# The second mixer of a three-block kernel, issued in another order: convolution inputs among the latents and queries, forward transforms among the keys, the keys' norms last

## The chip, the cores and the metric

The kernel runs on one core of a Trainium2 chip. The metric is device time in microseconds (us) of one execution; the time given for a kernel is the median of several runs.

## The reference, cut to what matters

Three blocks are chained over one sequence of 512 positions with 1024 features, all in float32. The change lies in the first half of the second block, its mixer: latent attention with 8 heads beside a long convolution (Hyena), both from the same normed input. In short:

```python
def second_block(x, ...):
    h = _rmsnorm(x, norm_mix)
    c_q, c_kv, k_pe, u_h = split(h @ w_in)            # 768, 256, 32, 1536 columns
    q = (_rmsnorm(c_q, q_norm) @ w_uq)                # 8 heads x 96
    kv = (_rmsnorm(c_kv, kv_norm) @ w_ukv)            # 8 heads x (64 key + 64 value)
    k = concat([k_nope, k_pe broadcast to the heads])
    q, k = _rmsnorm(q, qk_norm_q), _rmsnorm(k, qk_norm_k)   # per head, then rotary part
    y_attn = softmax(q k^T / sqrt(96)) v

    u_h = _dwconv3(u_h, short_conv_w, short_conv_b)   # 3-tap convolution over time
    x0, x1, vh = split(u_h, 3)                        # 512 columns each
    y_hyena = x0 * _bidir_long_conv(x1 * vh, h_fwd, h_bwd, bias)   # by rfft / irfft

    y_mix = concat([_rmsnorm(y_attn, ...), _rmsnorm(y_hyena, ...)])
    x = x + y_mix @ w_out
```

## The kernel before, in words

Activations are kept transposed, features on the 128 partitions and the 512 positions along the row, so that a tile is 128x512 and the stream x is 8 such tiles. Float32 products are made of three matmuls: both operands are split into a high part (rounded to the type that TensorE takes) and a low remainder, and wh·ah, wl·ah and wh·al are added up in one bank of PSUM. `proj_T` makes one 128-column tile of a projection so, with 8 x 3 = 24 matmuls of 128x512; `proj_N` makes tiles that have positions on the partitions, with matmuls of 128x256, and hands each half bank to an evacuation function. Both take their bank from a ring of three, called mm. `w()` loads the weights (512 KB by a DMA of SyncE's queue, SP), casts the high part on ScalarE (ACT, L110) and subtracts for the low part on VectorE (DVE, L111; on GpSimd, POOL, for the two convolution tiles in `UG`).

Ahead of the mixer, `TwoNorms.finish` (L1155) scales the 8 tiles of x on DVE (L1168) and writes each to a scratch in DRAM by a DMA of ACT's queue (L1171, 256 KB each); x's memory then goes back to the allocator, and the mixer's tiles are placed on it.

`mix2` has these steps, with the names used below:

- **latents**: two tiles ckv and six tiles cq by `proj_T`. Each is split with its gain (`split_scaled`: high part ACT L192, low part DVE L193), and ACT squares it (L1246 for the first tile, L1249 after it) for the norm's factor. Both readers use the bank itself. Between them stands kpe, one tile of 32 columns, which ACT copies out (L1271).
- **keys(g)**, four, and **queries(g)**, three: `proj_N` over ckv and cq; ACT evacuates keys and queries, DVE the values v (L1294).
- **wave(i)**, four: two convolution tiles, `uh(8+i)` and `uh(4+i)`, each a `proj_T` followed by a factor (`times`, DVE L249) and the 3-tap convolution (`conv3`: ACT L1133, DVE L1135 and L1136); then their product u (DVE L1357) and its write to DRAM. **turned(i)** transposes u on TensorE and splits it (ACT, DVE L1347). **gate0(i)**, four, is a convolution tile that is only written out.
- **norms** of q and k per head: ACT squares, DVE sums (L1317), a power on POOL (`rsqrt`: DVE L231, POOL L232), DVE scales (L1323, L1327). The rotary part is `rotate` (L1225 to L1227).
- **forward(f)**, two: 24 matmuls of 128x512 over the turned u, a mirror step on DVE (L1124, L1125), then the product with the filter's spectrum on DVE (L1388, L1389, L1391) and POOL, and splits (ACT L183, DVE L185) into Y. **inverse(j)** transforms back.
- **attention**: per head transposes of q and k (L1444) and their splits (L192, L193), scores (three matmuls per 128 rows), maxima on DVE (L1459), exponentials on ACT (L1461), transposes of the probabilities (L1474) and the values' matmuls.

Before, the order in the program is: ckv, kpe, cq, keys, queries; the waves, with a norm of q and k in each; rotation, gate0(0), gate0(1), turned(3); then the attention heads, behind which a list `fill` is written: gate0(2), gate0(3), forward(0), forward(1), inverse(0), inverse(1). Each engine executes its own instructions in the order of its list. That order is set when the kernel is built by a scheduler that takes the program's order as priority and its own idea of when inputs are ready, so a step that is written later can fill a wait of an earlier one. Tiles come from pools that open and close with a scope (`m2a` for latents, `m2b` for the turned u, `m2d` for attention); a tile that is placed on memory that another tile had waits until that one's last reader is done.

Of the kernel before, what the change touches and what calls it, by code (L numbers as in the profile page):

```python
# [10 lines left out]
F32 = mybir.dt.float32  # L11
# [6 lines left out]
P = 128  # L18
# [1173 lines left out]
def mix2(k, h, r12, bc, kf, xp, x1, done):  # L1192
# [3 lines left out]
    with k.tc.tile_pool(name="m2", bufs=1) as p:  # L1196
# [41 lines left out]
        with k.tc.tile_pool(name="m2a", bufs=1) as pa:  # L1238
            def latent(nm, n, g):
                out, acc = [], None  # L1240
                for i in range(n):
                    ps = k.proj_T([k.aps[nm][i]], h)
                    out.append(k.split_scaled(k.pair(pa, f"{nm}{i}"), ps, k.v(g, i)))
                    if acc is None:
                        acc = pa.tile([P, T], F32, tag=nm + "a", name=k.name("sa"))
                        S.activation(out=acc, in_=ps, func=AF.Square)  # L1246
                    else:
                        sq = tmp()
                        S.activation(out=sq, in_=ps, func=AF.Square)  # L1249
                        G.tensor_tensor(out=acc, in0=acc, in1=sq, op=ALU.add)  # L1250

                ss = k.small()
                V.tensor_tensor(out=ss, in0=r12, in1=r12, op=ALU.mult)
                V.tensor_tensor(out=ss, in0=ss, in1=k.col_sums(acc), op=ALU.mult)
                r = k.rsqrt(ss, NT, 1.0 / (n * P))
                o = p.tile([P, NT], F32, tag=nm + "r", name=k.name("lr"))
                V.tensor_tensor(out=o, in0=r, in1=r12, op=ALU.mult)
                return out, o

            ckv, rkv = latent("w2ckv", 2, "kv_norm")  # L1260

            hi, lo = k.w(k.aps["w2kpe"], 256)
            ps = k.bank()
            for i in range(NK):
                a, b = h[i]
                s = slice(i * 32, i * 32 + 32)
                k.mm(ps[0:32], hi[:, s], a, i == 0, False)
                k.mm(ps[0:32], lo[:, s], a, False, False)
                k.mm(ps[0:32], hi[:, s], b, False, i == NK - 1)
            kp = pa.tile([32, T], F32, tag="kp", name="kp")  # L1270
            S.copy(out=kp, in_=ps[0:32])  # L1271
            cq, rq = latent("w2cq", 6, "q_norm")
            ps = k.bank("t", 2)
            for t in range(NT):
                nc.tensor.transpose(ps[:, t * 32 : t * 32 + 32], kp[:, t * P : (t + 1) * P], k.ident[0:32, 0:32])
# [1062 lines left out]
```

## Time and profile before

| | |
|---|---|
| median of 3 runs | 2282.41 us (2281.33 to 2283.66) |
| profiled execution, its own time | 2280.31 us |
| its span (first to last instruction) | 2278.5 us |
| mean granted TensorE clock | 0.986 |
| TensorE matmuls (PE) busy | 2216.6 us, 97% of the span |
| DVE busy | 1391.8 us, 61% |
| ACT busy | 939.0 us, 41% |
| POOL busy | 534.1 us, 23% |

The second mixer lies, in this execution, between about 680 us and 970 us. Times in the rows are microseconds from the span's start unless they are marked ns. In rows of instructions, `[3.34 <-ACT P L1461]` means that the engine sat idle for 3.34 us until ACT's instruction of line 1461 had written P. PEclk is the granted clock as a share of the full one. A matmul's own time in the rows overlaps its neighbours'; how fast TensorE goes is read from the distance of their starts.

### The profile page before, as it was taken

The page shows a single profiled execution, that of the slowest core. Times are in us where ns is not written, and L with a number is a line of the kernel's source. Part 1 is how long each engine was busy: PE and PEld are TensorE (multiplying, and loading weights), DVE is VectorE, ACT ScalarE, POOL GpSimd, SP SyncE. Part 2 cuts the span into 40 slices and gives each one's busy share as a digit, 9 for nine tenths or more (in the row PEclk, how much of TensorE's full clock was granted, in tenths as well). Part 3 has the DMA queues.
Part 4 walks back from the last instruction along what each step waited for, and adds up shares of the span by engine and source line. Part 5 has one row for each costly group of instructions (what it writes and reads, how often), then busy time and mean ns, then how long its engine had stood idle before and what let it go on. Part 6 is the DMA issues. An engine that isn't in the chain of part 4 may idle for free.

```text
span 2278.5 us, 29275 instructions
## 1 busy us (share of the span) xinstructions
PE 2216.6 (97%) x11180; PEld 1822.6 (80%) x11180; DVE 1391.8 (61%) x2228; ACT 939.0 (41%) x1579; POOL 534.1 (23%) x459
## 2 busy tenths in 40 slices
PE   7899899999999998999999999999999999999998
PEld 3677789888888985678888887888888888888886
DVE  8775576654354598579647647977766664433433
ACT  4444455542243446544324334455444323222221
POOL 5232554431122225231101103000111211210320
PEclk8999999999999999999999999999999999999999
DMA  9552312122333342133232243212222322223222
GB/s 333 158 159 83 101 56 75 56 70 89 102 103 105 112 137 64 63 123 99 80 115 93 79 141 126 93 66 84 88 90 87 130 84 95 100 77 117 93 82 75
DMA packets 82164, 232.59 MB, mean 102 GB/s; under 512 B 10047, under 2 KB 10944, under 8 KB 82025
## 3 DMA queue, kind: packets, MB, share of 16 engines
q1 hardware_dynamic: 67208, 205.49, 28.0%
q10 hardware_dynamic: 14816, 25.25, 3.4%
q8 instruction: 88, 1.44, 0.3%
q14 instruction: 52, 0.42, 0.1%
HBM read 215.99 MB, written 15.22 MB: 101 GB/s over the span
## 4 chain that ended last, share of the span: by engine, by line
PE 56%; DVE 2%; issue 2%; ACT 1%; POOL 0%; POOLq 0%; DVEq 0%; ACTq 0%
PE mm L116 49%; PE s L116 3%; PE o L116 2%; PE t L116 1%; DVE sg L1634 0%; PE t L1474 0%; ACT wh L110 0%; DVE wl L111 0%; DVE x L2304 0%; DVE B L193 0%; DVE x L1635 0%; DVE st L1459 0%; PE t L1989 0%; ACT A L192 0%; PE t L1952 0%
## 5 line engine op out<-in xcount | busy, mean ns | idle before, releaser
L116 PE MATMUL mm<-A,wh 128*128 128x512 f32 (+1 forms) x2192 | 693.2, 392 | 4.8 <-ACT k L702 3.8
L110 ACT CAST wh<-wr 128x1024 fp32r<-128x1024 f32 (+3 forms) x370 | 363.4, 984 | 630.6 <-PE mm L116 416.0
L111 DVE TENSOR_TENSOR wl<-wr,wh 128x1024 fp32r<-128x1024 f32 (+3 forms) x366 | 438.0, 1198 | 282.4 <-ACT wh L110 280.4
L116 PE MATMUL mm<-B,wh 128*128 128x512 f32 x1688 | 541.9, 397 | 3.6 <-DVE B L193 2.1
L116 PEld LDWEIGHTS mm<-A,wh 128*128 128x128 f32 (+1 forms) x2192 | 409.8, 188 | 91.0 <-ACT k L702 4.1
L116 PE MATMUL mm<-A,wl 128*128 128x512 f32 (+1 forms) x1096 | 430.1, 393 | 1.1 <-DVE wl L111 1.1
L116 PEld LDWEIGHTS mm<-B,wh 128*128 128x128 f32 x1688 | 316.6, 188 | 75.4 <-DVE B L193 3.7
L116 PE MATMUL mm<-B,wl 128*128 128x512 f32 x844 | 332.4, 394 | 0.0
L116 PEld LDWEIGHTS mm<-A,wl 128*128 128x128 f32 (+1 forms) x1096 | 206.0, 188 | 44.0 <-DVE wl L111 1.9
L116 PEld LDWEIGHTS mm<-B,wl 128*128 128x128 f32 x844 | 159.0, 188 | 34.0 <-issue 1.2
L116 PE MATMUL mm<-a,wh 128*128 128x512 f32 x448 | 140.4, 389 | 0.0
L232 POOL TENSOR_TENSOR r<-r,mhalf 128x4 f32<-128x4 f32 (+1 forms) x40 | 53.1, 1330 | 351.9 <-DVE r L231 351.9
L249 DVE TENSOR_TENSOR us<-mm,bc 128x512 f32<-128x512 f32 x95 | 65.2, 689 | 93.6 <-PE mm L116 92.6
L185 POOL TENSOR_TENSOR a<-sl,a 128x512 fp32r<-128x512 f32 x28 | 40.5, 1446 | 274.2 <-ACT a L183 274.2
L116 PEld LDWEIGHTS mm<-a,wh 128*128 128x128 f32 x448 | 84.1, 188 | 17.4
L116 PE MATMUL mm<-a,wl 128*128 128x512 f32 x224 | 86.8, 389 | 0.0
L116 PE MATMUL mm<-wh,A 128*128 128x256 f32 x448 | 84.6, 285 | 0.0
L116 PEld LDWEIGHTS mm<-wh,A 128*128 128x128 f32 x448 | 70.7, 191 | 1.1 <-issue 0.6
L2224 POOL TENSOR_TENSOR sl<-sl,bc 128x512 f32<-128x512 f32 x22 | 28.7, 1305 | 167.6 <-DVE sl L1580 167.6
L116 PE MATMUL mm<-wl,A 128*128 128x256 f32 x224 | 63.7, 285 | 1.0 <-DVE wl L111 1.0
L734 ACT ACTIVATE d<-d 128x512 f32<-128x512 f32 x56 | 35.1, 629 | 68.4 <-POOL d L733 68.4
L1609 DVE TENSOR_TENSOR x<-x,mm 128x512 f32<-128x512 f32 x32 | 22.0, 687 | 64.5 <-PE mm L116 64.5
(584 smaller groups left out, 3568.6 us busy)
## 6 DMA issues: line engine op xcount, KB each, us to landing
wr<-w2upg SPq DMA_DIRECT2D x22, 512.0 KB, 3.4
wr<-w2upu SPq DMA_DIRECT2D x22, 512.0 KB, 3.5
wr<-w3fg SPq DMA_DIRECT2D x22, 512.0 KB, 3.4
wr<-w3fu SPq DMA_DIRECT2D x22, 512.0 KB, 3.4
adar<-w1ada SPq DMA_DIRECT2D x32, 256.0 KB, 5.1
wr<-w3out SPq DMA_DIRECT2D x16, 512.0 KB, 3.5
wr<-w2uh SPq DMA_DIRECT2D x12, 512.0 KB, 3.5
wr<-w2dn SPq DMA_DIRECT2D x16, 384.0 KB, 3.0
```

The costliest lines, as they stand in the source:

```text
L110: nc.scalar.copy(out=hi[:, :n], in_=r[:, :n])
L111: (eng or nc.vector).tensor_tensor(out=lo[:, :n], in0=r[:, :n], in1=hi[:, :n].bitcast(F32), op=ALU.subtract)
L116: return self.nc.tensor.matmul(out, a, b, start=start, stop=stop)
L185: eng.tensor_tensor(out=l[:p], in0=src, in1=hi[:p].bitcast(F32), op=ALU.subtract)
L232: nc.gpsimd.tensor_tensor(out=r, in0=r, in1=self.mhalf[:, :n], op=ALU.pow)
L249: self.nc.vector.tensor_tensor(out=out, in0=ps, in1=bc, op=ALU.mult)
L734: nc.scalar.activation(out=d, in_=d, func=AF.Exp)
L1609: k.nc.vector.tensor_tensor(out=xs[n], in0=xs[n], in1=ps, op=ALU.add)
L2224: nc.gpsimd.tensor_tensor(out=s, in0=s, in1=norm.bc, op=ALU.mult)
```

## The change

The same instructions are issued in another order; the arithmetic is the same. The pool `m2b` is opened ahead of `m2a`, and `latent` becomes a class whose tiles and whose norm factor can be issued apart.

```diff
         un = [None] * NT
+        bp = k.ctx2.enter_context(k.tc.tile_pool(name="m2b", bufs=1))
+        B = lambda i: k.pair(bp, f"B{i}")
...
         with k.tc.tile_pool(name="m2a", bufs=1) as pa:
...
-            ckv, rkv = latent("w2ckv", 2, "kv_norm")
+            lkv, lq = Latent("w2ckv", 2, "kv_norm"), Latent("w2cq", 6, "q_norm")
+            lkv.tiles(2)
...
             S.copy(out=kp, in_=ps[0:32])
-            cq, rq = latent("w2cq", 6, "q_norm")
+            lq.tiles(3)
+            wave(0)
+            lq.tiles(3)
...
+            ckv, cq = lkv.out, lq.out
+            rkv, rq = lkv.factor(), lq.factor()
...
+            wave(1)
+            queries(0)
+            wave(2)
+            queries(1)
+            wave(3)
+            queries(2)
+            gate0(0)
+            normed(qh, 96, None)
+            for i in range(1, 4):
+                gate0(i)
+            rotate(qh[:, :, :, 64:80], qh[:, :, :, 80:96], tabs[0], 8)
+            turned(3, us[3])
+            keys(0)
+            keys(1)
+            forward(0)
+            keys(2)
+            keys(3)
+            normed(kt, 64, kpr)
+            forward(1)
+
         with k.tc.tile_pool(name="m2d", bufs=1) as pd:
...
             fill = [
-                lambda: gate0(2),
-                lambda: gate0(3),
-                lambda: forward(0),
-                lambda: forward(1),
                 lambda: inverse(0),
                 lambda: inverse(1),
             ]
```

`normed` makes the norms of all four row tiles of q, or of k, in two pairs; `wave`, `gate0`, `turned` and `forward` are the same code as before, moved up.

In the following rows each line is one instruction in an engine's list: line of the program, operation, output and inputs, size, and in brackets which engines or DMA queues it waits for.

ACT at the start of the mixer, before. `scr_x` is the scratch that the x tiles are written to, `bc` a broadcast factor that scales them:

```order
L192 ACTIVATE w2ckv_6050<-mm_6019,vec 128x512 [waits PE_49]
L110 CAST wh_6143<-wr_6141 128x1024 [waits DMAHW6_49]
L1246 ACTIVATE sa_6054<-mm_6019 128x512 [waits DVE_49]
L192 ACTIVATE w2ckv_6087<-mm_6056,vec 128x512 [waits PE_49]
L110 CAST wh_6180<-wr_6178 128x1024 [waits DMAHW7_49]
L1249 ACTIVATE tmp_6091<-mm_6056 128x512 [waits DVE_49]
L244 COPY bc_5969<-t_5964 128x512 [waits PE_49]
L244 COPY bc_5976<-t_5971 128x512 [waits PE_49]
L1171 DMA scr_x<-x_4687 128x512 [waits DVE_49]
L1271 COPY kp<-mm_6113 32x512 [waits PE_49]
```

The same place in the changed kernel (its lines 1343, 1346 and 1371 are the lines 1246, 1249 and 1271 of before):

```order
L1171 DMA scr_x<-x_4699 128x512 [waits DMAHW2_49,DVE_49]
L1171 DMA scr_x<-x_4701 128x512 [waits DMAHW3_49,DVE_49]
L192 ACTIVATE w2ckv_6053<-mm_6022,vec 128x512 [waits DMAHW4_49,DMAHW3_49,DMAHW5_49,DMAHW2_49,DMAHW6_49,DMAHW1_49,DMAHW7_49,DMAHW0_49,Activation_49]
L192 ACTIVATE w2ckv_6090<-mm_6059,vec 128x512
L1371 COPY kp<-mm_6103 32x512
L1343 ACTIVATE sa_6057<-mm_6022 128x512 [waits DVE_49]
L1346 ACTIVATE tmp_6094<-mm_6059 128x512 [waits DVE_49]
L192 ACTIVATE w2cq_6161<-mm_6130,vec 128x512 [waits PE_49]
```

The splits and squares of both ckv tiles and the copy of kpe now stand behind all eight write-outs of x, and the first split waits for all DMA queues.

TensorE at the end of kpe (mm_6103) and the start of the first cq tile (mm_6130), in the changed kernel:

```order
L116 MATMUL mm_6103<-A_5930,wh_6099 32x512
L116 MATMUL mm_6103<-A_5930,wl_6100 32x512
L116 MATMUL mm_6103<-A_5931,wh_6099 32x512
L116 MATMUL mm_6130<-A_5638,wh_6133 128x512 [waits Activation_49]
L116 MATMUL mm_6130<-A_5638,wl_6134 128x512
```

The order is that of before here (and the wait for ACT too): ckv, ckv and kpe take the three banks, and the cq tile takes the one that is free first.

DVE around the first scores, before (kT and qT are a head's transposed keys and queries, st the maxima of its scores):

```order
L111 TENSOR_TENSOR wl_8367<-wr_8364,wh_8366 128x1024 [waits DMAHW7_49,Activation_49]
L1135 SCALAR_TENSOR_TENSOR tmp_8186<-tmp_8185,vec,tmp_8186 128x511 [waits DMAHW0_49,Activation_49]
L1136 SCALAR_TENSOR_TENSOR tmp_8186<-tmp_8185,vec,tmp_8186 128x511 [waits DVE_49]
L193 SCALAR_TENSOR_TENSOR kT_7404<-t_7398,vec,kT_7403 96x512 [waits Activation_49]
L1124 TENSOR_TENSOR tmp_8221<-tmp_8220,mm_8213 128x512 [waits DMAHW6_49,PE_49,Activation_49]
L193 SCALAR_TENSOR_TENSOR qT_7448<-t_7442,gs,qT_7447 96x512 [waits Activation_49]
L1125 TENSOR_TENSOR tmp_8220<-tmp_8220,mm_8213 128x512 [waits DVE_49]
L1388 TENSOR_TENSOR ft_8244<-tmp_8220,tmp_8198 128x512 [waits DMAHW7_49,DVE_49]
L1459 TENSOR_REDUCE st_7413<-s_7414 128x1 [waits PE_49]
```

The same place in the changed kernel (L1255 and L1259 scale the keys, L1314, L1315 and L1317 are forward's products):

```order
L185 TENSOR_TENSOR A_7395<-ft_7379,A_7394 128x512 [waits Activation_49]
L1124 TENSOR_TENSOR tmp_7592<-tmp_7591,mm_7584 128x512 [waits PE_49]
L1255 TENSOR_TENSOR k<-k,r_7526 128x8x64 [waits Pool_49]
L1259 TENSOR_TENSOR k<-kpr,r_7526 128x8x32
L1314 TENSOR_TENSOR ft_7596<-tmp_7572,tmp_7550 128x512 [waits DMAHW6_49,DVE_49]
L111 TENSOR_TENSOR wl_8454<-wr_8451,wh_8453 128x1024 [waits DMAHW2_49,Activation_49]
L1125 TENSOR_TENSOR tmp_7591<-tmp_7591,mm_7584 128x512 [waits DVE_49]
L1255 TENSOR_TENSOR k<-k,r_7537 128x8x64 [waits Pool_49]
L1259 TENSOR_TENSOR k<-kpr,r_7537 128x8x32
L1315 TENSOR_TENSOR tmp_7550<-tmp_7591,tmp_7550 128x512 [waits DVE_49]
L1317 TENSOR_TENSOR tmp_7591<-tmp_7591,tmp_7551 128x512 [waits DMAHW7_49,DVE_49]
L193 SCALAR_TENSOR_TENSOR kT_7650<-t_7644,vec,kT_7649 96x512 [waits Activation_49]
```

In the order before, the first head's kT stands ahead of what DVE does for the two forward transforms; in the changed order all of forward(0), the mirror steps of forward(1) and the scaling of all four key tiles stand ahead of it. From the L249 of gate0(0) to this kT, DVE's list in the changed kernel has, beside it: 6 L111 of 128x1024 and 4 of 128x512; 4 each of L249, L1135 and L1136; 16 sums of the norms (8 of q, 8 of k) and 4 scalings each of q, of k and of k's rotary part; 4 instructions of the rotation; 16 evacuations of v; 8 mirror steps; 3 each of L1314 (two of them into ft), L1315 and L1317; 4 L185; 2 qT; and 17 short ones (4 low halves of the turned u and 13 of 8 columns or fewer).

More of the change, by code (lines that the diff above doesn't have):

```diff
@@ new lines, in turned @@
+        def turned(i, u):
+            ps = k.bank("t", 2)
+            for t in range(NT):
+                nc.tensor.transpose(ps[:, t * P : (t + 1) * P], u[:, t * P : (t + 1) * P], k.ident)
+            for t in range(NT):
+                if i == 0:
+                    un[t] = B(t)
+                s = slice(i * P, (i + 1) * P)
+                S.copy(out=un[t][0][:, s], in_=ps[:, t * P : (t + 1) * P])
+                V.tensor_tensor(
+                    out=un[t][1][:, s], in0=ps[:, t * P : (t + 1) * P], in1=un[t][0][:, s].bitcast(F32), op=ALU.subtract
+                )
@@ new lines, in mix2, with wave, normed @@
+        us = []
+        def wave(i):
+            a, b = uh(8 + i), uh(4 + i)
+            u = tmp()
+            V.tensor_tensor(out=halved(u), in0=turns(a), in1=turns(b), op=ALU.mult)
+            S.dma_start(out=su[i], in_=u)
+            us.append(u)
+            if i:
+                turned(i - 1, us[i - 1])
+        def normed(x, w, pe):
+            for t in range(0, NT, 2):
+                rs = [head_sums(x, w, pe, t + i) for i in range(2)]
+                for i in range(2):
+                    head_scale(x, w, pe, t + i, rs[i])
```

218 lines of the change are left out of this document (95 added, 123 removed).

## The prediction, on record before the result was known

> **What bounds the kernel now.** I read the page first: over the span TensorE (PE) is busy for 97%, so a change of order can only win or lose the few places where it is not. Then a table of windows over the second mixer, whose columns are the stretch, its length, the busy time (and count) of PE, PE's weight loads, DVE, ACT and POOL, then the granted clock and DMA:
>
> ```profile
> 688.00:775.00 87.00, 87.00 (x555) 77.24 (x555) 36.83 (x71) 36.15 (x66) 16.98 (x14) 1.00 0.33 107
> 775.00:836.00 61.00, 61.00 (x280) 50.45 (x279) 56.06 (x102) 27.61 (x51) 23.14 (x11) 1.00 0.37 121
> 836.00:900.00 64.00, 54.39 (x256) 37.34 (x255) 57.94 (x78) 39.34 (x80) 28.17 (x20) 0.92 0.32 99
> 900.00:968.00 68.00, 64.76 (x369) 47.24 (x369) 37.11 (x52) 40.19 (x78) 16.61 (x12) 1.00 0.19 63
> ```
>
> Latents, keys and queries (688 to 775) leave DVE idle more than half the time and PE never. From the waves to the third head (775 to 900) DVE is busy for 56.06 + 57.94 = 114.0 of 125 us: that stretch is DVE's, and in its second half PE stands for 64 - 54.39 = 9.6 us. After 900 it stands for 3.2 us more. One of these gaps is long enough to halve the clock. The next rows are two gaps of PE from the timeline (and between them the first scores), and windows of 4 us behind each gap:
>
> ```profile
> 74.81 1.84 PE L116 MATMUL mm<-ones,ada 128*128 128x1 f32 x8 [6.08 <-DVE ada L425]
> ...
> 844.61 0.63 PE L116 MATMUL s<-kT,qT 96*128 96x512 f32 x2
> ...
> 887.56 1.65 PE L116 MATMUL s<-kT,qT 96*128 96x512 f32 x3 [3.34 <-ACT P L1461]
> ...
> 76.00:80.00 4.00, 4.00 (x16) 3.69 (x16) 0.73 (x2) 1.32 (x3) 0.00 (x0) 0.50 0.41 131
> 80.00:84.00 4.00, 4.00 (x14) 2.34 (x12) 2.83 (x5) 4.00 (x8) 0.00 (x0) 0.75 0.00 0
> ...
> 892.00:896.00 4.00, 3.54 (x11) 2.46 (x11) 3.50 (x6) 3.04 (x7) 2.60 (x3) 0.50 0.29 113
> 896.00:900.00 4.00, 4.00 (x16) 1.60 (x15) 2.40 (x4) 1.72 (x4) 0.00 (x0) 0.78 0.00 0
> ```
>
> After 6.08 us of standing, PE runs at half clock from 74.8 until about 82 (0.75 over 80 to 84 is half of it at half): 7.2 us, in which 3.6 us of work are lost. After 3.34 us it does so from 887.6 to about 898, and 5 us are lost. So the mixer loses 9.6 + 3.2 + 5 = 17.8 us of PE's time; that is all the change can win, unless other places move.
>
> **Part 1: the first split of ckv now waits for the write-outs of x.** The same wait exists before, on another tile. ACT's timeline, with `x6` six write-outs in a row:
>
> ```profile
> 686.97 0.69 ACT L192 ACTIVATE w2ckv<-mm,vec 128x512 fp32r<-128x512 f32 x1 [3.38 <-PE mm L116]
> ...
> 688.49 0.60 ACT L1246 ACTIVATE sa<-mm 128x512 f32<-128x512 f32 x1
> ...
> 699.97 0.58 ACT L1271 COPY kp<-mm 32x512 f32<-32x512 f32 x1 [1.26 <-PE mm L116]
> ...
> 700.86 3.64 ACTq L1171 DMA_DIRECT2D scr_x<-x  x6
> ...
> 706.38 0.69 ACT L192 ACTIVATE w2cq<-mm,vec 128x512 fp32r<-128x512 f32 x1 [4.88 <-DMA scr_x<-x]
> ```
>
> Before, ckv is split at once (686.97), and only the first cq tile falls on x's memory: its split stands until 706.38, when the last write-out has landed. That costs nothing, because the ckv banks are free by then and PE has banks for the next tiles. In the change, the pool of the turned u is opened first and takes the memory that ckv had; ckv lands on x's, and ACT's list puts both ckv splits, the kpe copy and the squares behind the eight write-outs. PE has filled three banks (ckv, ckv, kpe) at about 700.0, where kpe ends now, and its next matmul waits for ACT to give one back. ACT starts at 706.4 and has the two splits and the copy ahead of the square that is the first bank's last reader. Splits follow each other as the rows of the copies do, in about 0.6 us, so the bank is free after 3 x 0.6 + 0.6 = 2.4 us, at 708.8. Weights for the next tile are there by then. PE stands from 700.0 to 708.7: **+8.7 us**. Bounds: 7.0 if the square goes ahead of the others, 9.2 if PE arrives half a microsecond earlier, since the sums for ckv's norm are made later. DVE's and POOL's lists wait for the same data and gain nothing from it.
>
> Nothing hides the clock behind this gap, since PE is at 100% from here to 811. By the row of the 6.08 us gap I take 7.2 us at half clock: **+3.6 us**, between 0 and the 5 of the other gap. The Trainium skill, TensorE: Matmul & The Clock Gate, section What's actually happening, has the full clock back after about 3.4 us of sustained work; by it the term would be an estimated 1.7 us. The trace differs: both gaps are followed by twice that or more.
>
> **Part 2: the stretch that DVE sets.** PE's distances first: two latent tiles of 24 matmuls start their splits 5.44 us apart (0.227 a matmul), and a matmul of 128x256 takes 0.12.
>
> ```profile
> 711.82 0.69 ACT L192 ACTIVATE w2cq<-mm,vec 128x512 fp32r<-128x512 f32 x1 [3.31 <-PE mm L116]
> ...
> 717.26 0.69 ACT L192 ACTIVATE w2cq<-mm,vec 128x512 fp32r<-128x512 f32 x1 [3.31 <-PE mm L116]
> ...
> 900.54 0.28 PE L116 MATMUL mm<-wh,A 128*128 128x256 f32 x1
> 900.66 0.28 PE L116 MATMUL mm<-wl,A 128*128 128x256 f32 x1
> ```
>
> On a clock without part 1, PE does six cq tiles, eight wave tiles and gate0(0) (15 x 5.45 = 81.8), 216 query matmuls (25.9) and some 2 us of transposes between 700 and 810. The waves' DVE work (8 convolution tiles and the rest) now lies here, beside DVE time that was idle: at 36.83 of 87 us before, there is room, and I cost it at nothing. If the cover were gone it would show as PE waiting for a bank there.
>
> At 810 DVE takes the bank of gate0(0). What stands in its list from there to the first head's kT, without which the scores can't be finished, is priced by these groups (mean ns of one behind the busy time):
>
> ```profile
> L111 DVE TENSOR_TENSOR wl<-wr,wh 128x1024 fp32r<-128x1024 f32 x29 | 40.3, 1393 | 10.2 <-ACT wh L110 10.0
> L1135 DVE SCALAR_TENSOR_TENSOR tmp<-tmp,vec,tmp 128x511 f32<-128x511 f32 x12 | 9.6, 803 | 0.9 <-ACT tmp L1133 0.9
> L1136 DVE SCALAR_TENSOR_TENSOR tmp<-tmp,vec,tmp 128x511 f32<-128x511 f32 x12 | 8.9, 740 | 0.0
> L249 DVE TENSOR_TENSOR tmp<-mm,bc 128x512 f32<-128x512 f32 x12 | 8.2, 682 | 1.7 <-PE mm L116 1.7
> L185 DVE TENSOR_TENSOR A<-tmp,A 128x512 fp32r<-128x512 f32 x6 | 6.7, 1118 | 0.6 <-ACT A L183 0.6
> L193 DVE SCALAR_TENSOR_TENSOR kT<-t,vec,kT 96x512 fp32r<-96x512 f32 x8 | 5.9, 740 | 0.7 <-ACT kT L192 0.7
> L1294 DVE TENSOR_SCALAR v<-mm,lr 128x128 f32<-128x128 f32 x16 | 5.4, 347 | 2.3 <-ACT k L1291 2.2
> L1347 DVE TENSOR_TENSOR B<-t,B 128x128 fp32r<-128x128 f32 x16 | 4.5, 280 | 0.0
> L1389 DVE TENSOR_TENSOR tmp<-tmp,tmp 128x512 f32<-128x512 f32 x4 | 4.5, 1117 | 0.0
> L1317 DVE TENSOR_REDUCE sm<-tmp 128x4 f32<-128x384 f32 x8 | 4.0, 543 | 0.0
> L1323 DVE TENSOR_TENSOR q<-q,r 128x768 f32<-128x768 f32 x4 | 3.8, 953 | 1.1 <-POOL r L232 1.1
> L1391 DVE TENSOR_TENSOR tmp<-tmp,tmp 128x512 f32<-128x512 f32 x4 | 3.8, 946 | 0.0
> L1388 DVE TENSOR_TENSOR tmp<-tmp,tmp 128x512 f32<-128x512 f32 x2 | 2.9, 1462 | 0.1
> L1317 DVE TENSOR_REDUCE sm<-tmp 128x4 f32<-128x256 f32 x8 | 2.9, 406 | 0.0
> L1323 DVE TENSOR_TENSOR k<-k,r 128x512 f32<-128x512 f32 x4 | 2.8, 689 | 0.4 <-POOL r L232 0.4
> L111 DVE TENSOR_TENSOR wl<-wr,wh 128x512 fp32r<-128x512 f32 x4 | 2.7, 683 | 0.2 <-ACT wh L110 0.2
> L1124 DVE TENSOR_TENSOR tmp<-tmp,mm 128x512 f32<-128x512 f32 x4 | 2.7, 679 | 1.7 <-DMA scr_x<-tmp 1.7
> L1225 DVE TENSOR_TENSOR tmp<-q,tab 128x512 f32<-128x512 f32 x2 | 2.2, 1130 | 0.0
> L1327 DVE TENSOR_TENSOR k<-kpr,r 128x256 f32<-128x256 f32 x4 | 1.7, 417 | 0.0
> L1388 DVE TENSOR_TENSOR ft<-tmp,tmp 128x512 f32<-128x512 f32 x2 | 1.4, 688 | 0.0
> ```
>
> Weights 6 x 1.393 + 4 x 0.683 = 11.1; four gates' L249, L1135, L1136 8.9; norm sums 8 x 0.543 + 8 x 0.406 = 7.6; scalings 4 x (0.953 + 0.689 + 0.417) = 8.2; rotation at most 4 x 1.130 = 4.5; v 16 x 0.347 = 5.6; mirror 8 x 0.679 = 5.4; products 2 x 0.688 + 1.462 + 3 x 1.117 + 3 x 0.946 = 9.0; splits 4 x 1.118 = 4.5; two qT and kT at 0.740, 2.2; 17 short ones at most 0.280, 4.8. Sum 71.8; the terms marked "at most" are too high by some 2, so I take 70. DVE also idles: 61 - 56.06 = 4.9 us in the first of its two stretches before, and I take the same. The first kT is there at 810 + 70 + 4.9 = 885. In that time PE has three gates (16.4), 96 key matmuls (11.5), 48 of the two forwards (10.9) and some 2.7 of transposes and of inverse(0): 41.5 us. It stands for 74.9 - 41.5 = 33.4 us, in pieces, as banks come free. For the heads behind it I take 3.2 us, what the window 900 to 968 lost: the forwards are out of the way, and the inverse and output matmuls are still there as filling. Loss 33.4 + 3.2 = 36.6 against 17.8 before: **+18.8 us**.
>
> What the change wins is in this sum (the waves are gone from DVE's stretch); what it pays is that everything left stands ahead of the scores, where before heads 0 to 2 ran beside it. Bounds: below, no idle of DVE, and no collisions of DVE with POOL. The pairs of rows show these: 1462 against 688 ns for the same product. With all of L185, L1388, L1389 and L1391 at 688 the sum falls by 1.7 + 0.8 + 1.3 + 0.8 = 4.6, and by another 2 if the short ones are shorter still: 63.4 - 41.5 + 3.2 - 17.8 = +7. Above, the heads lose what 836 to 900 lost and the half clock too (9.6 + 5): +33. I stay near the middle. The Trainium skill, SBUF - State Buffer, section SBUF: two separate sides, has a two-input VectorE operation and a GpSimd one exclude each other for a whole instruction; the trace agrees (774 ns more), and by this rule forward's ten POOL operations beside the keys would keep the durations near the upper rows.
>
> **Sum.** 8.7 + 3.6 + 18.8 = 31.1. The profiled execution took 2280.31 us, so it would be 2311.4; it lies 2.1 below the median of the runs shown, so the forecast is **2313 us**.
>
> **Rivals.** (a) Only part 1 happens, and DVE's stretch comes out even: +12.3, 2295. For it: the windows show 17.8 us to win, and the waves take much from DVE. Against it: the list ahead of kT. (b) Only part 2 happens: if ckv's first split doesn't wait for x's landing, or a bank comes free otherwise: +18.8, 2301. Against it stands the list, with its wait for all queues. (c) Worse: the key norms' powers queue on POOL behind forward(0)'s ten operations, or the scores start behind a gap of over 3.3 us and lose another 5 us to the clock in a stretch that is then PE's: +33 and more with 12.3, 2328 or above. (d) The other side: DVE's stretch disappears as a bound. It decides from the point where DVE's list from gate0(0) to kT is shorter than PE's 41.5 us plus what PE lost before; then the 17.8 us come back, less the 3.2 of the heads: -14.6, which gives 2268 if part 1 doesn't happen, and 2280 (no change) if it does. For it: DVE was 92% busy just there and 26 us of wave work leave. Against it: 70 is far from 59. (e) The order on the engines isn't what the code says: the lists show that it is.
>
> **How the numbers follow.** Main case 0.55; (a) 0.12, (b) 0.10, (c) 0.08, (d) without part 1 0.09, with part 1 0.06. A measurement of this kernel can tell some 0.2%, 4.6 us, from no change. Faster: 0.09. Within: 0.06. Slower: 0.85. The range leaves out (d), 0.15, and the far end of (c), 0.05: from 2290, which takes in (a) with its bounds, to 2328, which the main case reaches when the heads lose as much as before. The main case by itself runs from 2300 (7 of part 2, 10 of part 1) to 2328.
>
> **What would show it.** A single wait of PE of 8 to 9 us behind kpe, at about 700, ended by ACT's square of ckv, with PEclk at 0.5 for some 7 us after; DVE at 90% or more from gate0(0) to the first scores, those about 50 us later than the 844.61 of before, with PE's time in that stretch in pieces; and hardly a wait in the heads after it. I am wrong if PE runs through at 700, if the first scores come before 880, or if the sum of PE's waits in the mixer is not some 25 us above that of before.

## The result and the profile after

The changed kernel takes 2319.28 us (median; 2318.61 to 2322.35), the kernel before 2282.58 us beside it: a ratio of 1.0163, with a 95% interval of 1.0149 to 1.0176. It is slower by some 37 us; the forecast was 2313.

The longest wait of TensorE that was not there before, and the windows of the mixer. The columns of the windows are those of the prediction (stretch, length, busy time of PE, PE's weight loads, DVE, ACT, POOL, clock, DMA); first the changed kernel, then the kernel before over the same stretches:

```profile
PE mm L116 <- ACT kp L1371: 9.4, 1, 9.4
...
690.00:720.00 30.00, 20.58 (x88) 14.88 (x88) 11.15 (x22) 7.84 (x12) 3.31 (x3) 0.83 0.37 122
720.00:760.00 40.00, 40.00 (x183) 33.03 (x183) 18.45 (x24) 14.44 (x20) 10.89 (x8) 1.00 0.31 93
...
840.00:860.00 20.00, 15.75 (x86) 13.71 (x86) 14.87 (x28) 7.90 (x19) 4.77 (x3) 0.83 0.52 159
860.00:880.00 20.00, 11.79 (x64) 9.16 (x62) 19.93 (x31) 9.42 (x22) 14.93 (x11) 0.88 0.26 82
880.00:900.00 20.00, 11.59 (x35) 7.37 (x36) 19.93 (x34) 6.49 (x11) 16.42 (x9) 0.59 0.26 89
```

```profile
690.00:720.00 30.00, 30.00 (x145) 23.33 (x144) 15.32 (x25) 11.19 (x16) 6.18 (x5) 1.00 0.38 132
840.00:860.00 20.00, 17.46 (x88) 13.46 (x86) 17.14 (x23) 10.64 (x21) 5.11 (x4) 1.00 0.50 161
860.00:880.00 20.00, 17.15 (x90) 10.50 (x90) 19.33 (x28) 14.48 (x31) 9.23 (x8) 1.00 0.23 65
880.00:900.00 20.00, 15.78 (x62) 10.08 (x62) 17.50 (x22) 11.64 (x24) 13.83 (x9) 0.74 0.20 57
```

Two places have grown. Between 700 and 720 TensorE stands for 9.42 us where it never stood. Between 840 and 900 it is busy for 39.1 us instead of 50.4, at a lower clock, while DVE is busy for 39.9 of 40 us from 860 on. The last matmul of attention ends at 967.8 before and at 1004.2 after, 36.4 us later (0.9 of it is there when the mixer begins); the spans, 2278.5 and 2316.8, differ by 38.3. From 680 us to that matmul TensorE loses, by standing and by half clock, 17.7 us before and 50.8 after. So the loss is in the mixer.

### The profile page after: what moved, and what is told of

Same layout as the page of the kernel before. It is cut to its first block, busy times and chain, and to the rows that moved or that the text cites. A ratio compares the mean times of both kernels' runs of the same rounds, so it can differ in the third digit from the quotient of the medians.

```text
span 2316.8 us, 29288 instructions
## 1 busy us (share of the span) xinstructions
PE 2229.7 (96%) x11180; PEld 1828.9 (79%) x11180; DVE 1392.7 (60%) x2228; ACT 941.8 (41%) x1579; POOL 540.1 (23%) x459
## 4 chain that ended last, share of the span: by engine, by line
PE 56%; DVE 4%; issue 2%; POOL 1%; ACT 1%; DMA 1%; POOLq 0%; DVEq 0%; ACTq 0%
PE mm L116 48%; PE s L116 3%; PE o L116 2%; PE t L116 1%; DVE wl L111 1%; PE t L1507 0%; DMA tmp<-scr_u 0%; DVE sg L1663 0%; ACT wh L110 0%; POOL tmp L1458 0%; DVE x L2333 0%; DVE x L1664 0%; DVE qT L193 0%; PE t L1477 0%; DVE tmp L1317 0%
## 5 line engine op out<-in xcount | busy, mean ns | idle before, releaser
L111 DVE TENSOR_TENSOR wl<-wr,wh 128x1024 fp32r<-128x1024 f32 (+2 forms) x366 | 435.7, 1192 | 288.3 <-ACT wh L110 286.5
L249 DVE TENSOR_TENSOR us<-mm,bc 128x512 f32<-128x512 f32 x95 | 65.2, 689 | 94.1 <-PE mm L116 92.6
L185 POOL TENSOR_TENSOR a<-sl,a 128x512 fp32r<-128x512 f32 x28 | 40.5, 1448 | 274.2 <-ACT a L183 274.2
L116 PE MATMUL mm<-wh,B 128*128 128x256 f32 x320 | 60.8, 288 | 0.0
```

The costliest lines, as they stand in the source:

```text
L111: (eng or nc.vector).tensor_tensor(out=lo[:, :n], in0=r[:, :n], in1=hi[:, :n].bitcast(F32), op=ALU.subtract)
L116: return self.nc.tensor.matmul(out, a, b, start=start, stop=stop)
L185: eng.tensor_tensor(out=l[:p], in0=src, in1=hi[:p].bitcast(F32), op=ALU.subtract)
L249: self.nc.vector.tensor_tensor(out=out, in0=ps, in1=bc, op=ALU.mult)
```

## Part 1 of the prediction: the wait for x's write-outs

ACT's timeline of the changed kernel, and TensorE's first matmul of the first cq tile:

```profile
699.04 0.59 ACT L244 COPY bc<-t 128x512 f32<-128x512 f32 x1 [4.46 <-PE t L116]
...
701.34 4.96 ACTq L1171 DMA_DIRECT2D scr_x<-x  x8
708.47 1.27 ACT L192 ACTIVATE w2ckv<-mm,vec 128x512 fp32r<-128x512 f32 x2 [6.56 <-DMA scr_x<-x]
709.62 0.56 ACT L1371 COPY kp<-mm 32x512 f32<-32x512 f32 x1
710.09 0.58 ACT L1343 ACTIVATE sa<-mm 128x512 f32<-128x512 f32 x1
...
710.24 0.79 PE L116 MATMUL mm<-A,wh 128*128 128x512 f32 x1 [9.42 <-ACT kp L1371]
...
704.69:710.24 5.55, 0.00 (x1) 0.01 (x1) 3.44 (x5) 1.77 (x4) 0.00 (x0) 0.50 0.90 298
710.24:714.93 4.69, 4.69 (x11) 3.72 (x12) 0.36 (x1) 0.99 (x2) 1.28 (x1) 0.50 0.01 3
```

The split of ckv waits 6.56 us for the write-outs, as read from the lists. Three details differ from the forecast and in part cancel. The bank that comes free first is kpe's, after its copy at 709.62, not ckv's after the square: 0.5 us sooner. The factor that scales x is ready at 699.04 instead of 697.23, and the last write-out lands 2.1 us later (the split starts at 708.47, not at 706.38). And TensorE ends kpe 0.8 us later, at 700.82. The gap is 9.42 us (forecast 8.7). TensorE works at half clock from 710.24 to 714.93, 4.7 us in which 2.3 are lost (forecast 3.6). This is closer to the 3.4 us of the Trainium skill, TensorE: Matmul & The Clock Gate, section What's actually happening, than to the 7.2 us of the row I took; the traces have both 4.7 and 7.2, and the shorter one follows the longer gap. Together 11.7 us against 12.3.

Why the longer gap costs less clock can be read from the granted clock. In the rows above it is at half from 704.69 to 714.93, 10.2 us, of which 5.5 lie in the gap, where TensorE has nothing to do. The row of before from which the prediction took its 7.2 us has 10.2 us at half clock too, but only 3.1 of them lie in its gap of 6.08 us:

```profile
71.74:74.81 3.07, 0.00 (x0) 0.03 (x1) 3.00 (x5) 0.00 (x0) 0.00 (x0) 0.50 0.46 113
74.81:81.98 7.17, 7.17 (x25) 6.40 (x26) 3.71 (x6) 3.30 (x6) 0.00 (x0) 0.50 0.29 99
```

**e1** takes the wait away from the changed kernel:

```diff
-                        self.out.append(k.split_scaled(k.pair(pa, f"{nm}{i}"), ps, ...))
+                        self.out.append(k.split_scaled(B(4 + i) if nm == "w2ckv" else k.pair(pa, f"{nm}{i}"), ps, ...))
...
-                            self.acc = pa.tile([P, T], F32, tag=nm + "a", ...)
+                            self.acc = bp.tile([P, T], F32R, tag="B6h" if nm == "w2ckv" else "B6l", ...).bitcast(F32)
...
-            kp = pa.tile([32, T], F32, tag="kp", name="kp")
+            kp = bp.tile([P, T], F32R, tag="B7h", ...).bitcast(F32)[0:32]
```

> The changed kernel with ckv's splits, the sums of squares and kpe's copy on tiles of the turned u's pool that are idle until attention, so that none of them lies on x's memory; order of the steps and everything else as in the change. My theory (the wait for x's write-outs is a loss of its own, 9.4 us of standing and 2.2 us at half clock, in a stretch that TensorE sets): 2319.3 - 11.6 = 2307.7 us, no gap of TensorE behind kpe, the first scores some 11 us earlier. Rival (the time is set by VectorE's stretch alone and swallows the gap, or the wait moves to the first cq tile): within 3 us of 2319.3.

Measured: 2306.70 us, 12.6 less than the changed kernel (ratio to before 1.0107, 1.0091 to 1.0123); the two profiled executions differ by 9.7. The gap is gone and the first scores come 9.0 us earlier, although this execution reached kpe 3.9 us later (697.2 us; 693.3 in the changed kernel's). Counted from the first matmul of kpe, in the further text from kpe, they come 12.8 us earlier, and attention ends after 297.8 us instead of 310.9:

```profile
690.00:720.00 30.00, 30.00 (x150) 23.48 (x149) 14.09 (x23) 11.19 (x16) 6.56 (x5) 1.00 0.42 141
...
885.45 2.93 PE L116 MATMUL s<-kT,qT 96*128 96x512 f32 x6 [0.56 <-ACT kT L192]
```

**e2** puts the same wait alone into the kernel before, by opening the pool of the turned u first:

```diff
         un = [None] * NT
+        bp = k.ctx2.enter_context(k.tc.tile_pool(name="m2b", bufs=1))
+        B = lambda i: k.pair(bp, f"B{i}")
         with k.tc.tile_pool(name="m2a", bufs=1) as pa:
...
-        bp = k.ctx2.enter_context(k.tc.tile_pool(name="m2b", bufs=1))
-        B = lambda i: k.pair(bp, f"B{i}")
```

> The kernel before, with one edit: the pool of the turned u is opened ahead of the latents' pool; order of the steps unchanged. My theory: ckv lands on x's memory here too, and the gap of 9 to 10 us behind kpe with 2 to 4 us at half clock comes alone: 2282.6 + 11.6 = 2294.2 us, and nothing else in the mixer changes. Rival (the gap belongs to the new order of the steps, not to the pool): 2282.6 us.

```profile
708.21 0.79 PE L116 MATMUL mm<-A,wh 128*128 128x512 f32 x1 [9.42 <-ACT kp L1273]
```

Measured: 2290.49 us, a ratio of 1.0041 (1.0025 to 1.0058), which is 9.4 us, between 5.7 and 13.2; 11.7 lies in it, 0 does not. The gap has the same length to the hundredth. From kpe to the end of attention e2 takes 286.0 us, and the kernel before 275.4. So the wait of part 1 and its cost belong to the order in which two pools are opened, not to the order of the steps.

## Part 2: the list ahead of the first scores

DVE's timeline of the changed kernel at the two ends of the stretch that the prediction priced (the evacuation of gate0(0), and the first kT), and TensorE's waits in it:

```profile
823.98 0.69 DVE L249 TENSOR_TENSOR tmp<-mm,bc 128x512 f32<-128x512 f32 x1 [2.41 <-PE mm L116]
...
894.41 0.74 DVE L193 SCALAR_TENSOR_TENSOR kT<-t,vec,kT 96x512 fp32r<-96x512 f32 x1
...
848.30 1.09 PE L1477 MATMUL t<-ident,q 128*96 128x128 f32 x4 [3.27 <-DVE q L1227]
866.40 0.36 PE L116 MATMUL mm<-wh,w2ckv 128*128 128x256 f32 x1 [2.44 <-DVE v L1399]
877.07 0.76 PE L116 MATMUL mm<-B,wh 128*128 128x512 f32 x1 [5.43 <-DVE v L1399]
894.43 2.93 PE L116 MATMUL s<-kT,qT 96*128 96x512 f32 x6 [0.56 <-ACT kT L192]
899.32 1.65 PE L116 MATMUL s<-kT,qT 96*128 96x512 f32 x3 [1.96 <-ACT P L1494]
...
823.98:895.15 71.17, 52.27 (x247) 41.67 (x245) 64.59 (x112) 31.00 (x63) 40.28 (x23) 0.84 0.35 112
900.00:905.00 5.00, 4.98 (x16) 3.45 (x15) 2.60 (x4) 3.41 (x8) 5.00 (x5) 0.50 0.39 105
```

From the evacuation to the end of the first kT are 71.2 us, 64.6 of DVE busy and 6.6 idle (forecast 74.9: 70 busy and 4.9 idle). The stretch starts at 824.0, 2.3 us later than the 810 of the forecast with the 11.7 of part 1, and is 3.7 us shorter, so that kT is there at 895.2, 1.5 us from the forecast: these two errors cancel in part. TensorE stands in this stretch for 18.9 us and loses 7.2 more to half clock: 26.1 instead of 33.4. It is less because the stretch is 3.7 us shorter and because TensorE has 45.1 us of work in it at full clock (52.3 busy, less 7.2), where I had counted 41.5. Behind the first scores it is the other way: 8.1 us of waits and 4.8 of half clock (at 0.50 until 906), 12.9 us where I had put 3.2. In sum 39.0 lost in part 2, against 36.6.

To see which of the moved steps costs this, the next kernels move them one by one, all starting from e1.

**e3**: both forwards back to the filling list.

```diff
             keys(0)
             keys(1)
-            forward(0)
             keys(2)
             keys(3)
             normed(kt, 64, kpr)
-            forward(1)
...
             fill = [
+                lambda: forward(0),
+                lambda: forward(1),
                 lambda: inverse(0),
```

> The kernel of e1 with one more edit: forward(0) and forward(1) go back to the head of the list that fills the attention heads; keys, gates and norms stay where the change put them. My theory (everything that stands in VectorE's list between gate0(0) and the first head's kT is paid): that list falls from 71 us by some 21 us (mirror steps 5.4, products 9.0, splits 4.5, weights 2.8), TensorE's work in it by 10.9, and the heads get the forwards' VectorE work back; first scores 20 us earlier than in e1, of which the heads give back about half: 2297 us. Rival (keys and their norms alone set the first scores, forwards are hidden beside them): within 3 us of e1. Rival (only the forwards matter): 2283 us or less.

Measured: 2294.44 us (1.0053, 1.0037 to 1.0069), 12.3 less than e1; forecast 9.7.

**e6**: the forwards stay ahead of the heads, but behind the keys' norms.

```diff
-            forward(0)
             keys(2)
             keys(3)
             normed(kt, 64, kpr)
+            forward(0)
             forward(1)
```

> The kernel of e1 with one edit: keys(2), keys(3) and the keys' norms stand ahead of forward(0) and forward(1), which are still issued before the heads. VectorE's list ahead of the first kT is 14 instructions and 14 us shorter (the same rows priced), TensorE's work ahead of it shrinks less. My theory (the list ahead of the first kT is paid, what is moved behind it is paid in part by the heads): first scores 12 us earlier than in e1, and 4 to 9 us of it kept: 2300 us. Rival (only the sum of VectorE's work before the second head counts): within 2 us of 2306.7. Rival (the keys' norms behind forward(0) are all that matters): 2294 us or less.

Measured: 2296.38 us (1.0064, 1.0047 to 1.0080), 10.3 less than e1. The first scores of the two kernels, e3 and then e6:

```profile
862.94 0.73 PE L116 MATMUL s<-kT,qT 96*128 96x512 f32 x2 [0.67 <-ACT kT L192]
```

```profile
861.58 0.72 PE L116 MATMUL s<-kT,qT 96*128 96x512 f32 x2 [0.66 <-ACT kT L192]
```

Counted from kpe they come at the same time (169.4 and 169.3 us after its first matmul), 19 us earlier than in e1, and the two times lie within each other's spread (2292.88 to 2296.37, 2293.16 to 2298.57). My expectation for e6 was too cautious by 4 us in time and by 7 us in the first scores: once the keys' norms are ahead, the scheduler itself lets the forwards run beside the heads. So most of what the late forwards and norms cost is one thing, that the keys' norms stand behind forward(0); that was e6's last rival (2294 us or less), and it is right up to 2 us.

**e8**: one resource. The values are evacuated by ACT instead of DVE, everything else is e1.

```diff
-                        V.tensor_scalar(
-                            out=v[:, t, 2 * g : 2 * g + 2], in0=s[:, :, 64:128], scalar1=rkv[:, t : t + 1],
-                            scalar2=None, op0=ALU.mult,
-                        )
+                        S.activation(
+                            out=v[:, t, 2 * g : 2 * g + 2], in_=s[:, :, 64:128], func=AF.Copy, scale=rkv[:, t : t + 1]
+                        )
```

> The kernel of e1 with one edit: the 16 evacuations of the values are made by ScalarE instead of VectorE (5.4 us of VectorE's time, in the stretch between gate0(0) and the first scores). Order and arithmetic unchanged. My theory (VectorE's list sets this stretch, so a microsecond taken out of it is a microsecond of time): first scores 5 us earlier, 2301 us (2299 to 2304). Rival (banks or the clock or GpSimd's powers set it): within 2 us of 2306.7.

Measured: 2303.65 us (1.0096, 1.0081 to 1.0111), 3.1 less than e1: in the expected range, at its slow end, and the two intervals overlap. Counted from kpe, the first scores come 4.4 us earlier than in e1 (expected 5), and ahead of them TensorE loses 21.7 us instead of 26.3. In the heads it loses 16.5 instead of 12.7, and from kpe to the end of attention the two kernels take the same time, 297.7 and 297.8 us. Its waits also lie elsewhere:

```profile
876.05 2.76 PE L116 MATMUL s<-kT,qT 96*128 96x512 f32 x6
...
863.63 0.45 PE L1476 MATMUL t<-ident,k 128*96 128x128 f32 x1 [11.27 <-DVE k L1259]
```

One wait of 11.27 us for the scaled keys has taken the place of several for the values' banks. It supports DVE's list as the setter of the stretch ahead of the scores. That a microsecond out of the list is a microsecond of time, as I expected, it does not show: most of what is won ahead of the scores is lost again behind them.

**e12**: the waves back behind the queries.

```diff
-            lq.tiles(3)
-            wave(0)
-            lq.tiles(3)
+            lq.tiles(6)
...
-            wave(1)
-            queries(0)
-            wave(2)
-            queries(1)
-            wave(3)
-            queries(2)
+            queries(0)
+            queries(1)
+            queries(2)
+            for i in range(4):
+                wave(i)
```

> The kernel of e1 with one edit: all four waves stand behind the queries again, as before the change; gates, keys among the forwards and keys' norms last stay as the change put them. Priced by rows, a wave is 11.3 us of TensorE (48 matmuls at 0.227 and 4 transposes) and about 9.0 of VectorE (2 x (0.682 + 0.803 + 0.740), 0.685 for u, 1.1 for its low halves, 2 x 1.393 for weights, of which one tile in four is GpSimd's). My theory since e5 (a wave is cover: in a stretch that VectorE sets it brings more TensorE work than VectorE work, so to take the waves out of it costs some 2 us each): putting them back wins 5 to 9 us: 2300 us. Rival (the reason one would move them for: VectorE is relieved of 36 us there): slower than e1, 2310 us or more. Rival (the waves' place doesn't matter): within 3 us of 2306.7.

Measured: 2303.61 us (1.0097, 1.0081 to 1.0112), 3.1 less than e1. To take 36 us of DVE work out of the busy stretch has won nothing: with them back the kernel is not slower. That refutes the reason for which one would move them. It is not the 5 to 9 us faster that I expected either: from kpe to the end of attention e12 takes 297.5 us and e1 297.8, so the rival that the waves' place does not matter fits best.

## Orders that should have been better, and were not

**e4** keeps the waves early and makes the keys and both norms early too; two gates and the forwards go back among the heads.

```diff
-            wave(1)
-            queries(0)
...
-            normed(kt, 64, kpr)
-            forward(1)
+            keys(0)
+            wave(1)
+            keys(1)
+            queries(0)
+            wave(2)
+            keys(2)
+            queries(1)
+            wave(3)
+            keys(3)
+            queries(2)
+            normed(kt, 64, kpr)
+            gate0(0)
+            normed(qh, 96, None)
+            gate0(1)
+            rotate(...)
+            turned(3, us[3])
...
             fill = [
+                lambda: gate0(2),
+                lambda: gate0(3),
+                lambda: forward(0),
+                lambda: forward(1),
```

> The kernel of e1 with the order: keys(0) wave(1) keys(1) queries(0) wave(2) keys(2) queries(1) wave(3) keys(3) queries(2), keys' norms, gate0(0), queries' norms, gate0(1), rotation, turned(3); gate0(2), gate0(3), forward(0), forward(1) at the head of the filling list as before the change. So the waves stay early, and what the change put late is early too. My theory: VectorE has room in the stretch that TensorE sets (37 of 87 us), so the list ahead of the first kT is short, hardly a wait before the first scores, and the heads lose less than before since no convolution tile of the waves is left: 2275 us (2268 to 2281). Rival (VectorE's total work is the bound, whatever the order): 2283 us or more.

Measured: 2287.83 us (1.0026, 1.0016 to 1.0035). Of e1's distance to before, 24 us, 19 are gone, but it is 5 slower than before and not 8 faster, so the expectation failed.

**e5** puts two waves and two gates around the norms, and the other two gates around the rotation:

```diff
+            for j, step in enumerate((lambda: wave(2), lambda: wave(3), lambda: gate0(0), lambda: gate0(1))):
+                fs = [head_sums(*norms[2 * j]), head_sums(*norms[2 * j + 1])]
+                step()
+                for i in range(2):
+                    head_scale(*norms[2 * j + i], fs[i])
+            gate0(2)
+            rotate(...)
+            gate0(3)
+            turned(3, us[3])
```

> The kernel of e1 with the order: wave(0) among the queries' latents, keys, wave(1), queries; then wave(2), wave(3), gate0(0), gate0(1), each with two norms (keys' first) issued around it, as the kernel before does around its four waves; gate0(2), rotation, gate0(3), turned(3); the forwards and inverses fill the heads. So as many convolution tiles as before cover the norms, and two gates less stand in the heads. My theory (what the change and e4 lost is the cover: a convolution tile gives TensorE 5.45 us of work beside some 3.6 of VectorE, and the norms, which are VectorE's alone, need it beside them): hardly a wait before the first scores, and the heads lose up to 7 us less than before: 2278 us (2274 to 2283). Rival (the heads' loss comes from the forwards alone, and with less filling they wait as long): 2283 us or more.

Measured: 2289.45 us (1.0028, 1.0015 to 1.0041). Failed again. Ahead of the first scores both kernels have a wait that I had not counted, e4's row first:

```profile
845.29 0.79 PE L116 MATMUL mm<-B,wh 128*128 128x512 f32 x1 [2.93 <-DVE tmp L249]
```

```profile
849.74 1.22 PE L116 MATMUL mm<-B,wh 128*128 128x512 f32 x2 [3.65 <-DVE B L1274]
...
860.00:880.00 20.00, 17.08 (x79) 12.19 (x78) 19.09 (x26) 11.02 (x26) 12.65 (x10) 0.91 0.26 75
880.00:900.00 20.00, 18.38 (x92) 11.11 (x91) 18.20 (x26) 12.97 (x27) 10.36 (x8) 0.92 0.17 58
```

forward(0) waits for a bank (e4) or for the last turned u (e5), which DVE's list has behind the queries' norms and the first half of the rotation. And in the heads DVE is as full as before (37.3 of 40 us in e5's rows), with two gates less in them.

**e10** therefore starts from the order before, moves only the queries behind wave(1), and with that the keys' norms into time in which DVE was idle; **e11** moves the last two gates out of the heads as well:

```diff
+            covered(0, lambda: wave(0))
+            covered(1, lambda: wave(1))
+            for g in range(3):
+                queries(g)
+            covered(2, lambda: wave(2))
+            covered(3, lambda: wave(3))
```

Here `covered(j, step)` issues two norms' sums, the step, and the two scalings.

> The order before, with the waves and the norms as pairs, and one step moved: the queries stand behind wave(1), so keys, wave(0), wave(1) with the keys' norms, queries, wave(2), wave(3) with the queries' norms; rotation, gate0(0), gate0(1), turned(3); gate0(2), gate0(3) and the forwards lead the filling list as before; ckv on idle tiles as in e1. What is moved ahead is the keys' norms (10.5 us of VectorE and nothing of TensorE) with two waves, into time in which VectorE was idle; what is moved back is the queries (25 us of TensorE, 6 of VectorE), the best cover there is. My theory: VectorE's backlog at the first scores is gone, and most of the 17.8 us that the mixer loses with it: 2274 us (2268 to 2280). Rival (the loss belongs to the heads' own chain, scores to maximum to exponential, and to the forwards inside them): 2281 us or more.

> The kernel of e10 with turned(3) ahead of the gates, and gate0(2) and gate0(3) ahead of the heads, so that only the forwards and inverses fill these. 7 us of VectorE and 10.9 of TensorE leave the heads. My theory (what stands in the heads delays their maxima, which release the scores): the heads lose some 3 to 5 us less than in e10, 2271 us. Rival (the gates are cover in the heads as the waves are before them): 2 to 4 us slower than e10.

Measured: e10 2284.85 us (1.0016, 1.0007 to 1.0025), e11 2283.92 us (1.0014, 1.0005 to 1.0022). Neither is faster than before, where I expected 2274 and 2271. In e10 there is no wait between 760 and the first scores, and still:

```profile
849.30 0.64 PE L116 MATMUL s<-kT,qT 96*128 96x512 f32 x2
...
867.78 0.79 PE L116 MATMUL s<-kT,qT 96*128 96x512 f32 x1 [1.39 <-ACT kT L192]
891.59 1.59 PE L116 MATMUL s<-kT,qT 96*128 96x512 f32 x3 [3.34 <-ACT P L1493]
```

The 3.34 us in front of a score that the prediction quoted of before stand here to the hundredth, and so does the 1.4 us wait for kT. So the mixer's loss before the change is not a backlog of the waves and norms, as I had read 114.0 of 125 us: from 775 to 836, DVE in e10 is busy for 39.0 us instead of 56.1, and the loss stays: TensorE loses 18.3 us against 17.7, and 14.7 of them behind the first scores. It is made in the heads, where DVE is as full as before (59.5 of 64 us from 836 to 900, against 57.9):

```profile
775.00:836.00 61.00, 61.00 (x370) 54.33 (x369) 39.03 (x61) 27.43 (x51) 16.00 (x8) 1.00 0.36 117
836.00:900.00 64.00, 55.98 (x271) 40.06 (x272) 59.48 (x83) 39.74 (x81) 28.65 (x20) 0.95 0.33 107
```

Around that wait, DVE in e10 has forward's product, a split of the attention's output and another product, and only then the maxima that release the exponentials:

```profile
885.66 1.10 DVE L1314 TENSOR_TENSOR tmp<-tmp,tmp 128x512 f32<-128x512 f32 x1
886.68 1.77 DVE L193 SCALAR_TENSOR_TENSOR B<-ya,vec,B 128x512 fp32r<-128x512 f32 x1
888.38 1.74 DVE L1315 TENSOR_TENSOR tmp<-tmp,tmp 128x512 f32<-128x512 f32 x1
890.04 1.27 DVE L1491 TENSOR_REDUCE st<-s 128x1 f32<-128x512 f32 x2
```

**e13** and **e14** take the forwards out of the heads once more, under the queries' matmuls; e14 leaves forward(1) in the heads.

```diff
             gate0(0) ... gate0(3)
             turned(3, us[3])
             forward(0)
             queries(0)
             queries(1)
-            forward(1)
             queries(2)
             normed(qh, 96, None)
             rotate(...)
...
             fill = [
+                lambda: forward(1),
                 lambda: inverse(0),
```

(Shown is the step from e13 to e14.)

> The forwards ahead of the heads as in the change, but with cover: latents, keys, wave(0) and wave(1) with the keys' norms, wave(2), wave(3), gate0(0) to gate0(3), turned(3), then forward(0), queries(0), queries(1), forward(1), queries(2), queries' norms, rotation, and the heads with both inverses as filling; ckv on idle tiles as in e1. The queries are 25 us of TensorE beside 6 of VectorE, and the forwards some 25 of VectorE beside 11 of TensorE, so together they are even; the inverse transforms (11.5 us of TensorE each half) cover the queries' norms. My theory (the change had the right step, forwards out of the heads, at a place without cover): waits ahead of the first scores below 8 us, heads lose less than 8 us instead of 17.8, 2276 us (2270 to 2282). Rival (the heads lose their 15 to 18 us by their own chain, whatever stands in them, as e10 and e11 might say): 2283 us or more, with the 3.3 us wait of a score for ACT's exponentials still there.

> The kernel of e13 with forward(1) behind the queries' norms, at the head of the filling list. It tells what one forward in the heads costs: my theory (VectorE's and GpSimd's work of a forward delays the heads' maxima): between e13 and e10, 3 to 6 us above e13, 2280 us. Rival (forward(1) would be cover there): at or below e13.

Measured: e13 2307.55 us (1.0106, 1.0089 to 1.0123), e14 2299.10 us (1.0073, 1.0057 to 1.0089). Both expectations failed, by some 30 and 20 us; e14 is 8.5 us below e13 and not above it, as its rival had it. The main waits of e13, and the one of e14:

```profile
869.30 0.58 PE L116 MATMUL mm<-wh,A 128*128 128x256 f32 x1 [3.41 <-ACT wh L110]
877.03 0.58 PE L116 MATMUL mm<-wh,A 128*128 128x256 f32 x1 [5.49 <-ACT A L183]
889.29 0.58 PE L116 MATMUL mm<-wl,A 128*128 128x256 f32 x1 [3.21 <-DVE wl L111]
```

```profile
872.68 1.09 PE L1478 MATMUL t<-ident,q 128*96 128x128 f32 x4 [11.03 <-DVE q L1227]
```

In e13 the inverse matmuls that should have covered the queries' norms wait themselves: the longest wait is for a split of Y (ACT), which is the end of the forward's chain, the two others for the splits of the inverse's own weights, which ACT's and DVE's lists have behind squares of the norms and behind the rotation. In e14 the transposes of q wait 11.03 us for the rotation. So these matmuls were no cover for the chains that stood in the same lists. Read with e10, the times go one way: 3 us above before with no forward ahead of the heads, 16 with one, 25 with two; the three orders also differ in where waves, gates and norms stand, so this is no price of one forward.

The heads themselves do gain when the forwards leave them. From the first score to the last matmul of attention, in e11 (two forwards among the heads), e14 (one) and e13 (none):

```profile
850.01:970.61 120.60, 107.82 (x584) 75.52 (x581) 85.80 (x116) 73.84 (x149) 45.13 (x32) 0.99 0.20 69
877.63:986.37 108.74, 100.02 (x551) 69.52 (x549) 69.31 (x98) 68.97 (x141) 27.91 (x21) 0.98 0.17 54
897.36:993.82 96.46, 89.22 (x456) 56.52 (x456) 53.53 (x82) 60.76 (x130) 13.15 (x10) 1.00 0.09 33
```

TensorE stands there for 12.8, 8.7 and 7.2 us, and with half clock loses 14.5, 10.4 and 7.2. So e13's expectation held for the heads (less than 8 us) and failed ahead of them: from 690 to the first score the three kernels lose 3.6, 21.2 and 27.1 us.

No kernel tried beats the one before.

## Why the prediction was right, and where it was off

- **What bounds the kernel.** That the mixer loses 17.8 us, and that more can be lost than won there, held. That this loss comes from all of DVE's stretch from the waves on did not hold: e10 relieves its first half, ahead of the scores, and keeps the loss; by e11, e14 and e13 a part of it goes with the forwards' work among the heads. No term of the sum rests on it, but the rival (d) and the expectations of e4, e5 and e10 do.
- **Part 1, +12.3 (8.7 and 3.6).** Measured 11.7 in the trace (9.4 and 2.3), 12.6 by e1, 5.7 to 13.2 by e2. Mechanism and place as forecast; the bank that ended the wait was kpe's, not ckv's. That the gap was forecast within 0.7 us is partly luck, since the later write-outs cancel against the earlier bank and the later end of kpe; the clock term came out too long because 5.5 us of the half clock fell into the gap.
- **Part 2, +18.8.** The list ahead of the first kT: forecast 74.9, measured 71.2. The term "For the heads behind it I take 3.2 us" was mis-sized: 12.9 measured, 4.8 of it half clock that the gaps around the first scores leave behind, and the sign "hardly a wait in the heads after it" did not come. The term of 33.4 ahead of them was 26.1. That the two errors nearly cancel, 39.0 instead of 36.6, is luck: the mechanism was right, and the closeness of the sum is better than that of its terms.
- **The rest.** 11.7 + 39.0 - 17.8 = 32.9 of the 36.4 us by which attention ends later. 0.9 of the remainder is older than the mixer. The other 2.6 us lie in no wait and in no half clock: from kpe to the end of attention TensorE issues the same 1431 matmuls, and they take 260.1 us of full clock instead of 257.6. Why is open.
- **"The waves' DVE work ... I cost it at nothing"** held: no wait of TensorE from 720 to 800.
- **Rivals.** (a), (b) and (d) fell with e1 to e3. Of (c), the powers behind forward(0) and the half clock behind the first scores are both in the trace, inside the main case.
- **Shares.** From the changed kernel back: the pool 12.6 us (e1), the forwards ahead of the keys' norms 12.3 (e3; 10.3 by e6). The last 11.8, from e3 to before, lies in the gates, queries' norms, keys and keys' norms that stand together behind the waves: e4, which makes keys and norms early and puts two gates back among the heads, takes 6.6 of it. How it divides further is open; e5 and e10 refute my accounts of it. Counted in the profiled executions from kpe to the end of attention, where nothing outside the mixer enters, the three shares are 13.1, 9.7 (11.2 by e6) and 12.7 us, so the shares are good to some 3 us.

## What to carry to other kernels

Opening a pool earlier can move other tiles onto memory that is still being written out, and the wait then appears on an engine that has nothing to do with either pool: compare who waits for DMA queues in the two lists. What decided here was the list ahead of the first instruction that the bottleneck needs; priced row by row it came within some 5% (74.9 against 71.2 us), while total load per stretch gave the wrong answer in e4, e5, e10 and e13. Work that ends in a chain over several engines (a power on GpSimd, a cast, a split) belongs where the bottleneck has independent work. Here that was the attention heads: the forwards cost them 7.3 us (e11 against e13) and 23.5 us ahead of them, though these two orders differ in more than the forwards.

## What the runs showed of the hardware that I had not expected

Instructions of DVE on 8 columns took up to 1.19 us beside GpSimd work, against 0.22 before the change. DVE's row in the changed kernel, GpSimd's at that time, and DVE's row before:

```profile
L1251 DVE TENSOR_SCALAR sm<-sm,pss x4: 213/586/1185, 871.8 to 881.8; 128x8 f32<-128x8 f32 x4
...
871.72 1.27 POOL L1318 TENSOR_TENSOR tmp<-tmp,tmp 128x512 f32<-128x512 f32 x1 [0.22 <-issue]
```

```profile
L1319 DVE TENSOR_SCALAR sm<-sm,pss x4: 215/218/221, 782.4 to 795.1; 128x8 f32<-128x8 f32 x4
```

The longest of the four starts 0.1 us behind this GpSimd instruction and is stretched to about its length, so the prediction's "17 short ones at most 0.280" was no upper bound. And TensorE worked at half clock for 4.7 us after a gap of 9.42, but for 7.2 after one of 6.08, because the half clock had begun 3.9 and 3.0 us into the gaps and lasted 10.2 us in both. After the 3.34 us of before it also lasted 10.2 us (887.52 to 897.76), nearly all of it on work. The length is not the same everywhere: after a gap of 3.27 us in the changed kernel it was 6.8 us (848.05 to 854.88).
